# A softmax over rows: ScalarE's exponential loops with one row a turn instead of five, and a shorter general path

## Chip, cores and metric

The kernel runs on one core of one Trainium2 chip. The metric is the device time of one execution in microseconds (us), taken as the median of several executions. The profile is a hardware trace of one execution.

## What is computed

A softmax with temperature 2 over the last axis of a float32 array of 16 x 1024 x 512, which the kernel treats as 16384 rows of 512 values:

```python
def reference(x: np.ndarray) -> np.ndarray:
    temp = 2.0
    x_scaled = x / temp
    x_max = np.max(x_scaled, axis=-1, keepdims=True)
    exp_x = np.exp(x_scaled - x_max)
    return (exp_x / np.sum(exp_x, axis=-1, keepdims=True)).astype(np.float32)
```

The input is drawn from a normal distribution. 33.55 MB are read and 33.55 MB are written.

## The kernel before

The 16384 rows lie on 128 partitions, so that each partition has 128 rows of 512 values ("row" means one such row of all partitions from here on). They are moved in ten tiles of 3, 5 and then eight times 15 rows. An arena in SBUF holds 98 rows; the first eight tiles fill it, and the last two go where tiles 0 to 3 were, once those are stored.

The fast path leaves the subtraction of the maximum out: ScalarE computes exp(0.5 x) in place, with the sum of each row as a second output, VectorE takes the reciprocal of the sums and multiplies, and SyncE stores. At the end VectorE and TensorE count how many sums lie between 1 and 1e30. If all do, the kernel is done; if not, a general path computes everything again with the maximum subtracted. With this input the general path's loops are not entered.

```python
TILES = [
    (3, 0), (5, 3), (15, 8), (15, 23), (15, 38), (15, 53), (15, 68), (15, 83), (15, 0), (15, 15),
]
LATE = {8: (0, 1, 2), 9: (3,)}     # tiles 8 and 9 are loaded when these are stored
ARENA = 98
HEAD = [3]
E = 5
TURN = 83
...
    def take(eng, sem, n):
        eng.wait_ge(sem, n).then_inc(sem, -n)
...
        # VectorE: one pair of instructions per tile, five rows at a time in the last tile
        for j, ks in enumerate(pairs):
            b, c = starts[ks[0]], sum(sizes[k] for k in ks)
            a = b % ARENA
            nc.vector.reciprocal(
                out=recip[:, b : b + c], in_=stats[:, b : b + c]
            )._wait_ge(s_exp, ks[-1] + 1).then_inc(s_rec, 1)
            nc.vector.tensor_mul(
                out=arena[:, a : a + c],
                in0=arena[:, a : a + c],
                in1=recip[:, b : b + c].unsqueeze(2).to_broadcast([P, c, D]),
            )._wait_ge(s_rec, j + 1).then_inc(s_mul, 1)
...
        # TensorE's queue waits for each load and tells ScalarE how many chunks it brought
        for t in range(len(tiles)):
            nc.tensor.wait_ge(ld[t], 48 if t == SPREAD else 16).then_inc(s_go, owner.count(t))
...
        nc.scalar.preload_act_table(Exp)
        for k, c in enumerate(HEAD):
            take(nc.scalar, s_go, 1)
            for b in range(starts[k], starts[k] + c):
                ins = nc.scalar.activation(
                    out=arena[:, b], in_=arena[:, b], func=Exp, scale=0.5,
                    accum_out=stats[:, b : b + 1],
                )
            ins.then_inc(s_exp, 1)
        exponentials(straight, TURN)            # rows 3 to 82
        for t, us in LATE.items():              # the loads of tiles 8 and 9
            nc.scalar.wait_ge(s_home[t], landings(us))
            load(nc.scalar, t)
        exponentials(TURN, n_rows)              # rows 83 to 127

        for t in range(len(tiles)):
            store(nc.sync, t)
...
    def exponentials(first, end):
        row = nc.scalar.alloc_register(f"row{first}")
        nc.scalar.reg_mov(row, first)
        with nc.scalar.While(lambda: nc.scalar.snap(row, min_val=first, max_val=end) < end):
            now = nc.scalar.snap(row, min_val=first, max_val=end - E)
            take(nc.scalar, s_go, 1)
            at = nc.s_assert_within(
                now % ARENA, 0, ARENA - E,
                skip_runtime_bounds_check_because="no chunk reaches over the arena's end",
            )
            for r in range(E):
                data = arena[:, r : ARENA - E + 1 + r][:, bass.ds(at, 1)]
                ins = nc.scalar.activation(
                    out=data, in_=data, func=Exp, scale=0.5,
                    accum_out=stats[:, r : n_rows - E + 1 + r][:, bass.ds(now, 1)],
                )
            ins.then_inc(s_exp, 1)
            nc.scalar.reg_add(row, row, E)
```

The loads of tiles 1 to 7 are issued by ScalarE ahead of all this, the load of tile 0 by SyncE. The general path of before works on 64 rows at a time, with a loop of one ACTIVATE a row on ScalarE.

Of the kernel before, what the change touches and what calls it, by code (L numbers as in the profile page):

```python
# [13 lines left out]
LATE = {8: (0, 1, 2), 9: (3,)}  # L14
ARENA = 98

HEAD = [3]
E = 5

SPREAD = 1  # L20

TURN = 83

LO, HI = 1.0, 1.0e30
G = 64
# [3 lines left out]
def kernel(  # L29
# [5 lines left out]
    nc = tc.nc  # L35
# [3 lines left out]
    Exp = mybir.ActivationFunctionType.Exp  # L39
    Alu = mybir.AluOpType  # L40
# [3 lines left out]
    N, D = xf.shape  # L44
    P = nc.NUM_PARTITIONS
    n_rows = N // P
    assert sum(r for r, _ in TILES) == n_rows

    arena = nc.alloc_sbuf_tensor("arena", (P, ARENA, D), fp32)
    stats = nc.alloc_sbuf_tensor("stats", (P, n_rows), fp32)  # L50
# [4 lines left out]
    flag = nc.alloc_sbuf_tensor("flag", (1, 1), mybir.dt.int32)  # L55
# [15 lines left out]
        _, r, at = tiles[t]  # L71
        return arena[:, at : at + r, :]

    straight = sum(HEAD)
    sizes = HEAD + [E] * ((n_rows - straight) // E)
    starts = [sum(sizes[:k]) for k in range(len(sizes))]
    assert sum(sizes) == n_rows
    owner = [max(t for t, (b, _, _) in enumerate(tiles) if b <= s) for s in starts]
    assert all(s + c <= sum(tiles[t][:2]) for s, c, t in zip(starts, sizes, owner))


    pairs = []
    for k, t in enumerate(owner):
        most = 1 if t == len(tiles) - 1 else 3
        if pairs and len(pairs[-1]) < most and owner[pairs[-1][0]] == t:
            pairs[-1].append(k)
        else:
            pairs.append([k])
    upto = [1 + max(j for j, ks in enumerate(pairs) if owner[ks[0]] == t) for t in range(len(tiles))]

    ld = [nc.alloc_semaphore(f"ld{t}") for t in range(len(tiles))]
    s_home = {t: nc.alloc_semaphore(f"s_home{t}") for t in LATE}
# [11 lines left out]
    g_go = nc.alloc_semaphore("g_go")  # L104
    g_top = nc.alloc_semaphore("g_top")
    g_st = nc.alloc_semaphore("g_st")
    g_neg = nc.alloc_semaphore("g_neg")
    g_exp = nc.alloc_semaphore("g_exp")
    g_rec = nc.alloc_semaphore("g_rec")
    g_mul = nc.alloc_semaphore("g_mul")  # L110
# [27 lines left out]
    def take(eng, sem, n):  # L138
        eng.wait_ge(sem, n).then_inc(sem, -n)  # L139

    def rounds(eng, body, step=1):

        last = n_rows // G
        i = eng.alloc_register("tile")
        eng.wait_ge(s_near, 16)
        eng.wait_ge(s_flag, 1)
        eng.reg_load(i, flag[0:1, 0:1])
        with eng.While(lambda: eng.snap(i, min_val=0, max_val=last) < last):  # L150
            body(eng.snap(i, min_val=0, max_val=last - 1))
            eng.reg_add(i, i, step)

    def early():
        load(nc.sync, 0)
# [5 lines left out]

    def program():

        for j, ks in enumerate(pairs):
            b, c = starts[ks[0]], sum(sizes[k] for k in ks)
            a = b % ARENA
            nc.vector.reciprocal(  # L167
                out=recip[:, b : b + c], in_=stats[:, b : b + c]
            )._wait_ge(s_exp, ks[-1] + 1).then_inc(s_rec, 1)
            nc.vector.tensor_mul(  # L170
                out=arena[:, a : a + c],
                in0=arena[:, a : a + c],
                in1=recip[:, b : b + c].unsqueeze(2).to_broadcast([P, c, D]),
            )._wait_ge(s_rec, j + 1).then_inc(s_mul, 1)

        nc.gpsimd.memset(ones[:, :], 1.0).then_inc(s_ones, 1)  # L176
        nc.gpsimd.tensor_scalar(  # L177
            out=inside[:, :], in0=stats[:, :], scalar1=LO, scalar2=HI,
            op0=Alu.max, op1=Alu.min,
        )._wait_ge(s_exp, len(sizes)).then_inc(s_cnt, 1)  # L180
        nc.vector.scalar_tensor_tensor(  # L181
            out=inside[:, :], in0=inside[:, :], scalar=1.0, in1=stats[:, :],
            op0=Alu.mult, op1=Alu.is_equal, accum_out=count[:, :],
        )._wait_ge(s_cnt, 1).then_inc(s_cnt, 1)
        nc.vector.tensor_scalar(  # L185
            out=flag[:, :], in0=total[:, :], scalar1=float(N), scalar2=float(n_rows // G),
            op0=Alu.is_ge, op1=Alu.mult,
        )._wait_ge(s_tot, 1).then_inc(s_flag, 1)


        for t in range(len(tiles)):
            nc.tensor.wait_ge(ld[t], 48 if t == SPREAD else 16).then_inc(s_go, owner.count(t))
        nc.tensor.wait_ge(s_ones, 1)
        nc.tensor.matmul(  # L194
            total[:, :], lhsT=count[:, :], rhs=ones[:, :], start=True, stop=True
        )._wait_ge(s_cnt, 2).then_inc(s_tot, 1)

        nc.scalar.preload_act_table(Exp)  # L198
        for k, c in enumerate(HEAD):
            take(nc.scalar, s_go, 1)  # L200
            for b in range(starts[k], starts[k] + c):
                ins = nc.scalar.activation(  # L202
                    out=arena[:, b], in_=arena[:, b], func=Exp, scale=0.5,
                    accum_out=stats[:, b : b + 1],
                )
            ins.then_inc(s_exp, 1)
        exponentials(straight, TURN)
        for t, us in LATE.items():
            nc.scalar.wait_ge(s_home[t], landings(us))
            load(nc.scalar, t)  # L210
        exponentials(TURN, n_rows)

        for t in range(len(tiles)):
            store(nc.sync, t)

        x_g = xf.rearrange("(t p r) d -> t p r d", p=P, r=G)
        o_g = of.rearrange("(t p r) d -> t p r d", p=P, r=G)
        data = arena[:, 0:G]  # L220

        def vector(_):
            for i in range(n_rows // G):
                nc.vector.reduce_max(
                    out=g_max[:, :], in_=data, axis=mybir.AxisListType.X, negate=True
                )._wait_ge(g_go, i + 1).then_inc(g_top, 1)
                nc.vector.reciprocal(
                    out=g_sum[:, :], in_=g_sum[:, :]
                )._wait_ge(g_exp, G * (i + 1)).then_inc(g_rec, 1)

        def scalar(_):
            take(nc.scalar, g_neg, 1)
            row = nc.scalar.alloc_register("g_row")
            nc.scalar.reg_mov(row, 0)
            with nc.scalar.While(lambda: nc.scalar.snap(row, min_val=0, max_val=G) < G):
                now = nc.scalar.snap(row, min_val=0, max_val=G - 1)
                nc.scalar.activation(
                    out=data[:, bass.ds(now, 1)], in_=data[:, bass.ds(now, 1)], func=Exp,
                    scale=0.5, bias=g_max[:, bass.ds(now, 1)], accum_out=g_sum[:, bass.ds(now, 1)],
                ).then_inc(g_exp, 1)  # L240
                nc.scalar.reg_add(row, row, 1)

        def gpsimd(_):
            nc.gpsimd.wait_ge(s_end, at_end)
            for i in range(n_rows // G):
                nc.gpsimd.dma_start(out=data, in_=x_g[i]).then_inc(g_ld, 16)
                nc.gpsimd.wait_ge(g_ld, 16 * (i + 1)).then_inc(g_go, 1)
                nc.gpsimd.tensor_scalar_mul(
                    out=g_max[:, :], in0=g_max[:, :], scalar1=0.5
                )._wait_ge(g_top, i + 1).then_inc(g_neg, 1)  # L250
                nc.gpsimd.tensor_mul(
                    out=data, in0=data, in1=g_sum[:, :].unsqueeze(2).to_broadcast([P, G, D])
                )._wait_ge(g_rec, i + 1).then_inc(g_mul, 1)
                nc.gpsimd.wait_ge(g_mul, i + 1)
                nc.gpsimd.dma_start(out=o_g[i], in_=data).then_inc(g_st, 16)
                nc.gpsimd.wait_ge(g_st, 16 * (i + 1))

        rounds(nc.vector, vector, n_rows // G)
        rounds(nc.scalar, scalar)
        rounds(nc.gpsimd, gpsimd, n_rows // G)  # L260
        nc.sync.wait_ge(s_near, 16)
        nc.sync.wait_ge(s_end, at_end)

    def exponentials(first, end):
        row = nc.scalar.alloc_register(f"row{first}")
        nc.scalar.reg_mov(row, first)
        with nc.scalar.While(lambda: nc.scalar.snap(row, min_val=first, max_val=end) < end):  # L267
            now = nc.scalar.snap(row, min_val=first, max_val=end - E)  # L268
            take(nc.scalar, s_go, 1)
            at = nc.s_assert_within(  # L270
                now % ARENA, 0, ARENA - E,
                skip_runtime_bounds_check_because="no chunk reaches over the arena's end",
            )
            for r in range(E):
                data = arena[:, r : ARENA - E + 1 + r][:, bass.ds(at, 1)]
                ins = nc.scalar.activation(  # L276
                    out=data, in_=data, func=Exp, scale=0.5,
                    accum_out=stats[:, r : n_rows - E + 1 + r][:, bass.ds(now, 1)],
                )
            ins.then_inc(s_exp, 1)  # L280
            nc.scalar.reg_add(row, row, E)

    here = str(nc.cur_bb)
    entry, rest = nc.main_func.blocks[0], list(nc.main_func.blocks[1:])
# [42 lines left out]
```

## Time and profile before

| | |
|---|---|
| median time | 159.96 us (lowest 159.89) |
| span of the profiled execution | 158.7 us |
| ScalarE busy | 80.6 us (51%) |
| VectorE busy | 73.2 us (46%) |
| moved by DMA | 67.12 MB, mean 423 GB/s over the span |
| idle time of ScalarE until a load had landed | 55.6 us |

An engine's busy time counts its data instructions; register, branch and semaphore instructions of its sequencer are recorded, but not counted as busy. "L276" is line 276 of the kernel. A name with q at its end (ACTq, SPq) is an engine's sequencer. Times are from the start of the span.

### The profile page before, as it was taken

The numbers are of one execution on the slowest core, as the hardware profiler recorded it, in microseconds if no ns is written. First come the engines' busy times: TensorE is split into PE (matmuls) and PEld (weight loads), VectorE is DVE, ScalarE is ACT, GpSimd is POOL, SyncE is SP. The second block draws the span as 40 slices with busy tenths as digits, with TensorE's granted clock in tenths as the row PEclk, the third lists the DMA queues.
The fourth block names the chain that finished last, engine by engine and source line by source line (L and its number), as shares of the span: only waits on it lengthen the run. The fifth ranks groups of instructions, "written<-read, shape, count | busy, mean of one in ns | idle before, by whom it ended". The sixth has DMA issues, their size and how long they took to land. (4 is left out here: it accounts for less than half of the span.)

```text
span 158.7 us, 659 instructions
## 1 busy us (share of the span) xinstructions
PE 0.2 (0%) x2; PEld 0.1 (0%) x2; DVE 73.2 (46%) x27; ACT 80.6 (51%) x257; POOL 0.9 (1%) x6
## 2 busy tenths in 40 slices
PE   0000000000000000000000000000000000000000
PEld 0000000000000000000000000000000000000000
DVE  0047001992981990059500991049700793796000
ACT  0590498697498009940399007950199205980000
POOL 0000000000000000000000000000000000010000
DMA  7999999989899999999999999999999999999995
GB/s 265 395 480 401 454 407 363 501 372 501 387 472 395 472 395 465 403 457 410 457 410 457 410 441 426 443 426 441 426 434 434 434 434 434 434 434 434 410 449 256
DMA packets 3025, 67.12 MB, mean 423 GB/s; under 512 B 336, under 2 KB 336, under 8 KB 720
## 3 DMA queue, kind: packets, MB, share of 16 engines
q1 hardware_dynamic: 1584, 34.34, 50.5%
q10 hardware_dynamic: 1440, 32.77, 48.5%
q14 instruction: 1, 0.01, 0.0%
HBM read 33.55 MB, written 33.55 MB: 423 GB/s over the span
## 5 line engine op out<-in xcount | busy, mean ns | idle before, releaser
L276 ACT ACTIVATE arena<-arena x125 | 76.6, 614 | 55.6 <-ACTq L139 55.6
L170 DVE TENSOR_TENSOR arena<-arena,recip 128x7680 f32<-128x7680 f32 (+2 forms) x12 | 70.2, 5847 | 0.4
L167 DVE RECIPROCAL recip<-stats 128x15 f32<-128x15 f32 (+2 forms) x12 | 2.7, 224 | 71.9 <-ACT arena L276 62.7
L276 ACT ACTIVATION_READ_ACCUMULATOR arena<-arena x125 | 23.3, 186 | 0.0
L198 ACT ACT_TABLE_LOAD x1 | 1.3, 1283 | 5.8 <-issue 5.8
L202 ACT ACTIVATE arena<-arena 128x512 f32<-128x512 f32 x3 | 1.9, 618 | 0.0
L177 POOL TENSOR_SCALAR inside<-stats 128x128 f32<-128x128 f32 x1 | 0.6, 634 | 139.4 <-ACT arena L276 139.4
L202 ACT ACTIVATION_READ_ACCUMULATOR arena<-arena 128x1 f32 x3 | 0.6, 187 | 0.0
L194 PE MATMUL total<-ones,count 128*1 128x1 f32 x2 | 0.2, 164 | 145.4 <-DVE inside L181 145.4
L181 DVE SCALAR_TENSOR_TENSOR inside<-inside,stats 128x128 f32<-128x128 f32 x1 | 0.3, 285 | 0.0
L185 DVE TENSOR_SCALAR flag<-total 1x1 int32<-1x1 f32 x1 | 0.1, 146 | 0.3 <-PE total L194 0.3
L194 PEld LDWEIGHTS total<-ones,count 128*1 128x1 f32 x2 | 0.1, 80 | 145.4 <-DVE inside L181 145.4
L176 POOL MEMSET ones<- 128x1 f32 x1 | 0.1, 98 | 2.2 <-POOLq L37 2.2
L311 POOL MEMSET const-bfloat16-1.0<- 128x1 bf16 x1 | 0.1, 102 | 0.0
L311 POOL MEMSET const-uint8-127<- 128x1 uint8 x1 | 0.1, 102 | 0.0
L311 POOL MEMSET const-float32-0.0<- 128x1 f32 x1 | 0.1, 99 | 0.2 <-issue 0.2
L311 POOL MEMSET const-float32-1.0<- 128x1 f32 x1 | 0.1, 99 | 0.0
L181 DVE DVE_READ_ACCUMULATOR inside<-inside,stats 128x1 f32 x1 | 0.1, 83 | 0.0
## 6 DMA issues: line engine op xcount, KB each, us to landing
arena<-in_x_dram ACTq DMA_DIRECT2D x8, 3840.0 KB, 42.9
out_dram<-arena SPq DMA_DIRECT2D x8, 3840.0 KB, 27.4
out_dram<-arena SPq DMA_DIRECT2D x1, 1280.0 KB, 23.5
arena<-in_x_dram ACTq DMA_DIRECT2D x1, 1024.0 KB
arena<-in_x_dram SPq DMA_DIRECT2D x1, 768.0 KB, 5.5
out_dram<-arena SPq DMA_DIRECT2D x1, 768.0 KB, 15.3
arena<-in_x_dram ACTq DMA_DIRECT2D x1, 252.0 KB
arena<-in_x_dram ACTq DMA_DIRECT2D x1, 4.0 KB
```

Source lines behind the costliest of these rows:

```text
L167: nc.vector.reciprocal(out=recip[:, b : b + c], in_=stats[:, b : b + c])._wait_ge(s_exp, ks[-1] + 1).then_inc(s_rec, 1)
L170: nc.vector.tensor_mul(out=arena[:, a : a + c], in0=arena[:, a : a + c], in1=recip[:, b : b + c].unsqueeze(2).to_broadcast([P, c, D]),)._w ...
L176: nc.gpsimd.memset(ones[:, :], 1.0).then_inc(s_ones, 1)
L177: nc.gpsimd.tensor_scalar(out=inside[:, :], in0=stats[:, :], scalar1=LO, scalar2=HI, op0=Alu.max, op1=Alu.min,)._wait_ge(s_exp, len(sizes) ...
L181: nc.vector.scalar_tensor_tensor(out=inside[:, :], in0=inside[:, :], scalar=1.0, in1=stats[:, :], op0=Alu.mult, op1=Alu.is_equal, accum_ou ...
L185: nc.vector.tensor_scalar(out=flag[:, :], in0=total[:, :], scalar1=float(N), scalar2=float(n_rows // G), op0=Alu.is_ge, op1=Alu.mult,)._wa ...
L194: nc.tensor.matmul(total[:, :], lhsT=count[:, :], rhs=ones[:, :], start=True, stop=True)._wait_ge(s_cnt, 2).then_inc(s_tot, 1)
L198: nc.scalar.preload_act_table(Exp)
L202: ins = nc.scalar.activation(out=arena[:, b], in_=arena[:, b], func=Exp, scale=0.5, accum_out=stats[:, b : b + 1],)
L276: ins = nc.scalar.activation(out=data, in_=data, func=Exp, scale=0.5, accum_out=stats[:, r : n_rows - E + 1 + r][:, bass.ds(now, 1)],)
L311: nc = _bacc.Bacc("TRN2", target_bir_lowering=False, num_devices=1)
```

## The change

The change makes ScalarE's program shorter, from 76 instructions to 48:

- The two loops of the fast path take one row a turn, not five. The semaphore from the loads to ScalarE counts rows, and so does the one from ScalarE to VectorE.
- The first three rows, which stood as instructions of their own, go into the first loop.
- VectorE's chunks are written down directly (a tile each, five rows each in the last tile). Their shapes and order are the same as before.
- In the general path ScalarE does 64 rows in one ACTIVATE, without a loop. For that GpSimd adds the negative maximum to the data first, and VectorE sums the rows. The loops run zero times or once.

```diff
-HEAD = [3]
 E = 5
...
+    chunks = []
+    for t, (b, r, _) in enumerate(tiles):
+        c = r if t < len(tiles) - 1 else E
+        assert r % c == 0
+        chunks += [(t, b + o, c) for o in range(0, r, c)]
...
-            )._wait_ge(s_exp, ks[-1] + 1).then_inc(s_rec, 1)
+            )._wait_ge(s_exp, b + c).then_inc(s_rec, 1)
...
-        )._wait_ge(s_exp, len(sizes)).then_inc(s_cnt, 1)
+        )._wait_ge(s_exp, n_rows).then_inc(s_cnt, 1)
...
-            nc.tensor.wait_ge(ld[t], 48 if t == SPREAD else 16).then_inc(s_go, owner.count(t))
+            nc.tensor.wait_ge(ld[t], 48 if t == SPREAD else 16).then_inc(s_go, tiles[t][1])
...
         nc.scalar.preload_act_table(Exp)
-        for k, c in enumerate(HEAD):
-            take(nc.scalar, s_go, 1)
-            for b in range(starts[k], starts[k] + c):
-                ins = nc.scalar.activation(
-                    out=arena[:, b], in_=arena[:, b], func=Exp, scale=0.5,
-                    accum_out=stats[:, b : b + 1],
-                )
-            ins.then_inc(s_exp, 1)
-        exponentials(straight, TURN)
+        exponentials(0, TURN)
...
-        def scalar(_):
-            take(nc.scalar, g_neg, 1)
-            row = nc.scalar.alloc_register("g_row")
-            ...
+        def scalar():
+            for i in range(n_rows // G):
+                nc.scalar.activation(out=data, in_=data, func=Exp, scale=0.5)._wait_ge(
+                    g_sub, i + 1
                 ).then_inc(g_exp, 1)
...
-            now = nc.scalar.snap(row, min_val=first, max_val=end - E)
+            now = nc.scalar.snap(row, min_val=first, max_val=end - 1)
             take(nc.scalar, s_go, 1)
-            at = nc.s_assert_within(
-                now % ARENA, 0, ARENA - E,
-                skip_runtime_bounds_check_because="no chunk reaches over the arena's end",
-            )
-            for r in range(E):
-                data = arena[:, r : ARENA - E + 1 + r][:, bass.ds(at, 1)]
-                ins = nc.scalar.activation(
-                    out=data, in_=data, func=Exp, scale=0.5,
-                    accum_out=stats[:, r : n_rows - E + 1 + r][:, bass.ds(now, 1)],
-                )
-            ins.then_inc(s_exp, 1)
-            nc.scalar.reg_add(row, row, E)
+            data = arena[:, bass.ds(now % ARENA, 1)]
+            nc.scalar.activation(
+                out=data, in_=data, func=Exp, scale=0.5, accum_out=stats[:, bass.ds(now, 1)]
+            ).then_inc(s_exp, 1)
+            nc.scalar.reg_add(row, row, 1)
```

More of the change, by code (lines that the diff above doesn't have):

```diff
@@ L72, in sb @@
         return arena[:, at : at + r, :]
[L74 to L89, printed above, removed]
+    chunks = []
[3 more added lines that the diff above has]
+        chunks += [(t, b + o, c) for o in range(0, r, c)]
+    upto = [1 + max(j for j, c in enumerate(chunks) if c[0] == t) for t in range(len(tiles))]
     ld = [nc.alloc_semaphore(f"ld{t}") for t in range(len(tiles))]
@@ L106 @@
     g_st = nc.alloc_semaphore("g_st")
-    g_neg = nc.alloc_semaphore("g_neg")
+    g_sub = nc.alloc_semaphore("g_sub")
+    g_add = nc.alloc_semaphore("g_add")
     g_exp = nc.alloc_semaphore("g_exp")
@@ L139, in take, with rounds @@
         eng.wait_ge(sem, n).then_inc(sem, -n)
-    def rounds(eng, body, step=1):
-        last = n_rows // G
-        i = eng.alloc_register("tile")
+    def rounds(eng, body):
+        i = eng.alloc_register("general")
         eng.wait_ge(s_near, 16)
@@ L149, in rounds @@
         eng.reg_load(i, flag[0:1, 0:1])
-        with eng.While(lambda: eng.snap(i, min_val=0, max_val=last) < last):
-            body(eng.snap(i, min_val=0, max_val=last - 1))
-            eng.reg_add(i, i, step)
+        with eng.While(lambda: eng.snap(i, min_val=0, max_val=1) < 1):
+            body()
+            eng.reg_add(i, i, 1)
     def early():
@@ L162, in program @@
     def program():
-        for j, ks in enumerate(pairs):
-            b, c = starts[ks[0]], sum(sizes[k] for k in ks)
+        for j, (_, b, c) in enumerate(chunks):
             a = b % ARENA
@@ L185, in program @@
         nc.vector.tensor_scalar(
-            out=flag[:, :], in0=total[:, :], scalar1=float(N), scalar2=float(n_rows // G),
-            op0=Alu.is_ge, op1=Alu.mult,
+            out=flag[:, :], in0=total[:, :], scalar1=float(N), scalar2=None, op0=Alu.is_ge,
         )._wait_ge(s_tot, 1).then_inc(s_flag, 1)
         for t in range(len(tiles)):
-            nc.tensor.wait_ge(ld[t], 48 if t == SPREAD else 16).then_inc(s_go, owner.count(t))
+            nc.tensor.wait_ge(ld[t], 48 if t == SPREAD else 16).then_inc(s_go, tiles[t][1])
         nc.tensor.wait_ge(s_ones, 1)
@@ L220, in program, with vector @@
         data = arena[:, 0:G]
-        def vector(_):
+        def vector():
             for i in range(n_rows // G):
@@ L226, in vector, with gpsimd @@
                 )._wait_ge(g_go, i + 1).then_inc(g_top, 1)
+                nc.vector.reduce_sum(
+                    out=g_sum[:, :], in_=data, axis=mybir.AxisListType.X
+                )._wait_ge(g_exp, i + 1).then_inc(g_add, 1)
                 nc.vector.reciprocal(
                     out=g_sum[:, :], in_=g_sum[:, :]
-                )._wait_ge(g_exp, G * (i + 1)).then_inc(g_rec, 1)
-        def scalar(_):
-            take(nc.scalar, g_neg, 1)
-            row = nc.scalar.alloc_register("g_row")
[L234 to L239, printed above, removed]
+                )._wait_ge(g_add, i + 1).then_inc(g_rec, 1)
+        def scalar():
+            for i in range(n_rows // G):
+                nc.scalar.activation(out=data, in_=data, func=Exp, scale=0.5)._wait_ge(
+                    g_sub, i + 1
                 ).then_inc(g_exp, 1)
-                nc.scalar.reg_add(row, row, 1)
-        def gpsimd(_):
+        def gpsimd():
             nc.gpsimd.wait_ge(s_end, at_end)
@@ L247, in gpsimd @@
                 nc.gpsimd.wait_ge(g_ld, 16 * (i + 1)).then_inc(g_go, 1)
-                nc.gpsimd.tensor_scalar_mul(
-                    out=g_max[:, :], in0=g_max[:, :], scalar1=0.5
-                )._wait_ge(g_top, i + 1).then_inc(g_neg, 1)
+                nc.gpsimd.tensor_add(
+                    out=data, in0=data, in1=g_max[:, :].unsqueeze(2).to_broadcast([P, G, D])
+                )._wait_ge(g_top, i + 1).then_inc(g_sub, 1)
                 nc.gpsimd.tensor_mul(
@@ L256, in gpsimd @@
                 nc.gpsimd.wait_ge(g_st, 16 * (i + 1))
-        rounds(nc.vector, vector, n_rows // G)
+        rounds(nc.vector, vector)
         rounds(nc.scalar, scalar)
-        rounds(nc.gpsimd, gpsimd, n_rows // G)
+        rounds(nc.gpsimd, gpsimd)
         nc.sync.wait_ge(s_near, 16)
```

## Prediction

> **What bounds the kernel now.** I read the page first, for which engine is full. Its slices (40 of 4 us each, busy share in tenths) show two half-empty compute engines and full DMA engines:
>
> ```profile
> span 158.7 us, 659 instructions
> ...
> DVE  0047001992981990059500991049700793796000
> ACT  0590498697498009940399007950199205980000
> ...
> DMA  7999999989899999999999999999999999999995
> ```
>
> ScalarE and VectorE have holes in every tile; the DMA row has none except in the first and the last slice. So I cut the span where transfers begin and end (columns: stretch, length, busy time of PE, PEld, DVE, ACT, POOL, TensorE clock, DMA share, GB/s):
>
> ```profile
> 0.00:1.00 1.00, 0.00 (x0) 0.00 (x0) 0.00 (x0) 0.00 (x0) 0.20 (x4) 1.00 0.00 0
> 1.00:2.00 1.00, 0.00 (x0) 0.00 (x0) 0.00 (x0) 0.00 (x0) 0.00 (x0) 1.00 0.92 283
> ...
> 11.00:132.40 121.40, 0.00 (x0) 0.00 (x0) 61.93 (x17) 66.14 (x214) 0.00 (x0) 1.00 1.00 431
> 132.40:157.40 25.00, 0.19 (x2) 0.09 (x2) 9.40 (x9) 9.30 (x30) 0.63 (x1) 1.00 1.00 433
> 157.40:158.70 1.30, 0.00 (x0) 0.00 (x0) 0.00 (x0) 0.00 (x0) 0.00 (x0) 1.00 0.01 0
> ```
>
> The first load is issued at 0.00, data moves from 1.0 us on, and until 157.4 the share is 1.00; then 1.3 us pass until the last landing is known. The kernel moves 67.12 MB; 156.4 us of it gives 429 GB/s, and no stretch is left in which more could be moved. The time is bytes over rate plus 1.0 us before and 1.3 us after. A change in ScalarE's program moves it only if it makes the DMA engines run dry, or changes those two ends.
>
> Next, what ScalarE's rows cost (the groups of instructions, columns: busy us and mean ns of one, then the idle time before them and its releaser):
>
> ```profile
> L276 ACT ACTIVATE arena<-arena x125 | 76.6, 614 | 55.6 <-ACTq L139 55.6
> L170 DVE TENSOR_TENSOR arena<-arena,recip 128x7680 f32<-128x7680 f32 x7 | 57.1, 8158 | 0.2
> L276 ACT ACTIVATION_READ_ACCUMULATOR arena<-arena x125 | 23.3, 186 | 0.0
> ```
>
> An exponential is an ACTIVATE of 0.614 us and a read of its sum of 0.186 us, which overlap their neighbours: in the timeline one row follows the next every 0.61 us, also across a turn of the loop. The 55.6 us idle are waits for loads (L139 is the wait on `s_go`). Last, the end, from the timeline and, for the loop's sequencer work, the chain of waits (start, length, what; L276 here is the register operation ahead of an activation, L267 the loop's test):
>
> ```profile
> 141.86 0.19 ACT L276 ACTIVATION_READ_ACCUMULATOR arena<-arena  x1
> ...
> 142.31 2.83 DVE L170 TENSOR_TENSOR arena<-arena,recip 128x2560 f32<-128x2560 f32 x1
> ...
> 145.16 0.33 SPq L136 DMA_DIRECT2D out_dram<-arena  x1
> ```
>
> ```profile
> 132.95 0.07 ACTq L276
> ...
> 133.12 0.07 ACTq L276
> ...
> 133.60 0.04 ACTq L267
> ...
> 133.81 0.03 ACTq L267
> ...
> 134.07 0.10 ACTq L276
> ...
> 134.26 0.07 ACTq L276
> ```
>
> [...] the loop's test at 133.60 to 133.87 lies beside an ACTIVATE that runs from 133.38 to 133.99, and no gap follows. [...] here the step from the first test to what follows it is 133.60 to 133.81, so 0.21 us for both[...]. [...] the sum of loads and stores stays at 431 to 433 GB/s here, whether both queues are active or stores alone[...].
>
> **The change, part by part.**
>
> *Turns of one row.* Before, a turn does five rows, so 25 turns and three rows without a loop; after, 128 turns. The sequencer's work of a turn of one row, from the chain above: register operation to next one 0.19 (134.07 to 134.26), then the add to the row register and the step from it, about 0.06 (as between the close steps of that chain), then from the first test to the next turn's register operation 0.47 (133.60 to 134.07; test, jump, test, copy of the row, wait on `s_go`). Sum 0.72 us in the second loop, where the arena index wraps. In the first loop the wraparound costs less: in tile 5 the wait on `s_go` starts at 59.6 and again at 60.9,
>
> ```profile
> L139 ACTq EVENT_SEMAPHORE  x2: 17/17/17, 59.6 to 60.9; - x2
> ```
>
> so a turn of five rows took 1.3 us of sequencer, four of its rows at 0.16 to 0.17 (132.95 to 133.12), which leaves 0.63 to 0.65 for a turn of one row. The engine needs 0.61 a row. So a turn of one row is just no longer hidden: the row's period becomes the larger of the two, 0.63 in the first loop and 0.72 in the second.
>
> *First loop, rows 0 to 82.* A tile of 15 rows lasts 14 x 0.02 = 0.3 us longer. Loads land every 18.1 us (ScalarE waits 8.9 us ahead of each of these tiles), ScalarE takes 9.2 and VectorE 8.4, so there is room. The store of a tile goes out 0.3 us later; but stores in mid-run take some 34 us from issue to landing, of which 18 is their own share, so each waits about 16 us behind another. Hidden. The loads of the last two tiles are issued by ScalarE after this loop, at 84.1. There the sequencer was some 3.5 us ahead of the engine; it will no longer be, so I expect 87.5. They are needed when the load before them has moved its data, just before it lands at 95.8 (issue at 5.3 and 90.5 us). Hidden, with 7 us to spare.
>
> *Second loop, the last tile.* This is the only place near the path. Its load lands at 132.4, and its store of 3.93 MB, issued at 145.16, ends the kernel. After: the fifteenth row ends 14 x (0.72 - 0.61) = 1.5 us later, at 143.5 in place of 142.0. VectorE's three chunks of 3.06 us had just kept pace with five rows of 3.06; with rows of 0.72 the third chunk starts at once after the fifteenth row and ends 3.05 us later, at about 146.7. So the last store is issued 1.5 us later. How much of that shows? The store's 3.93 MB at 433 GB/s take 9.1 us and end at 157.4, so its data begins at 148.3, behind the store before it. An issue on idle engines was followed by data after 1.0 us (first cut of the span). So issue at 147.3 would do: 2.1 us of slack, against 1.5 us. Hidden, with 0.6 us left.
>
> *No separate first rows.* ScalarE's first row starts at 7.10 after its table load (5.81 to 7.09), which waits behind nine DMA issues. The new loop's head, some 0.3 us of sequencer work, falls in the table load. Zero. Stores of the first two tiles go out up to 0.2 us later; loads keep the engines full.
>
> *VectorE, stores, loads.* Instruction by instruction the same shapes and order; only line numbers and the thresholds of the waits differ, in rows rather than chunks. *General path*: runs only when a sum is out of bounds, so here no instruction of it runs. Fewer instructions to fetch: nothing in the chain waits for a fetch. Zero.
>
> Sum: 0.0 on the path, plus a small allowance of 0.05: 160.0 us.
>
> **Rivals.** First, the sequencer doesn't run ahead over a branch, so that each turn's 0.47 us stands beside 0.61: rows of 1.1 us, a last tile 14 x 0.47 = 6.6 us longer, less 2.1 of slack, so 164.5. For it: per-row loops are the change's whole price. Against it: the timeline of before has no gap at any of its turns. Second, the turn is dearer than my 0.72 (a longer jump, a row's wait not ready): at 0.80 the store goes out 2.7 us later, and 0.6 us shows, 160.6. Third, the short loop jumps faster, so that rows come at 0.63 in both loops: the same 160.0, which only the trace would tell from my reading. Fourth, a shorter program starts sooner: against it, the first data moves at 1.0 us after two DMA issues that no part of the change touches. Fifth, ScalarE's later stores let loads run ahead, the balance of the queues shifts, and the rate with it; in the two mixes seen it is 431 and 433, so under 0.5%.
>
> **Range and chances.** The centre is 160.0. Below there is only scatter: 159.5. Above, the thin slack of 0.6 us can be used up by some turns of 0.75 to 0.80: 160.8. A slowdown of over 2%, 3.2 us, needs rows of 1.0 us, which is the first rival; I give it 3 in 100. A gain of over 2% would need the DMA engines to move faster: 1 in 100.
>
> **What would show it.** ACTIVATE still about 0.61 us, but row starts 0.63 apart up to row 82 and 0.72 in the last two or three tiles; ScalarE's wait for loads shorter by 0.3 to 1.5 us a tile; the loads of the last two tiles issued near 87.5; the last store near 146.7; DMA share 1.00 without a hole between 147 and 149. Wrong if the DMA share drops ahead of the last store, or if rows come at 1 us or more.

## The result and the profile after

The changed kernel takes 160.72 us against 159.93 us, each the median of six executions; the ratio is 1.0047, with a 95% interval of 1.0031 to 1.0063. A second set gave 160.57 against 159.90 us and 1.0046 (1.0033 to 1.0059). Some executions of most of these kernels take 5 to 14 us longer than the others of the same program; the ratios leave them out, and so do the medians of the second set and of the table below. So the loss is real, but small, some 0.7 us, and lies within the predicted range; the predicted centre, 160.0, was too low by most of it. The profile shown here is that of the second set, an execution of 160.57 us.

From its page (slices of 4 us, busy share in tenths; then the groups of instructions, with busy us, mean ns, and idle time before them):

```profile
span 159.2 us, 1279 instructions
...
DVE  0047001993971990059500990029800694787000
ACT  0590598796598009930499008970299305990000
...
DMA  7999998989898989898989898989899999999994
...
L247 ACT ACTIVATE arena<-arena x128 | 80.1, 627 | 53.3 <-ACTq L130 53.2
...
L247 ACT ACTIVATION_READ_ACCUMULATOR arena<-arena x128 | 24.0, 187 | 0.0
```

The program is shorter, yet the trace has 1279 instructions where it had 659: one row a turn means that the loop's own instructions run 128 times instead of 25. ScalarE's idle time until loads land fell from 55.6 to 53.3 us only, and VectorE is as before. The stretches of transfers, cut as before (ACT is the fourth busy column; the last three numbers are TensorE clock, DMA share and GB/s):

```profile
1.00:2.00 1.00, 0.00 (x0) 0.00 (x0) 0.00 (x0) 0.00 (x0) 0.00 (x0) 1.00 0.95 283
11.00:132.40 121.40, 0.00 (x0) 0.00 (x0) 61.29 (x17) 68.72 (x215) 0.00 (x0) 1.00 1.00 430
```

430 GB/s where it was 431, and the start is the same. So the 0.7 us is neither in the start nor in a visibly lower rate. The end, from the timeline:

```profile
142.85 0.19 ACT L247 ACTIVATION_READ_ACCUMULATOR arena<-arena  x1
143.07 0.19 DVE L155 RECIPROCAL recip<-stats 128x5 f32<-128x5 f32 x1 [0.29 <-ACT arena L247]
...
143.29 2.83 DVE L158 TENSOR_TENSOR arena<-arena,recip 128x2560 f32<-128x2560 f32 x1
...
146.14 0.33 SPq L127 DMA_DIRECT2D out_dram<-arena  x1
```

The last store is issued at 146.14 instead of 145.16, 0.98 us later. That is close to the loss, so it was the first suspect ("the end theory" below: the late store leaves the DMA engines without work ahead of its data); the next view speaks against it. After that issue there is no hole in the DMA engines:

```profile
146.14:147.00 0.86, 0.19 (x2) 0.09 (x2) 0.33 (x3) 0.00 (x0) 0.00 (x0) 1.00 0.83 357
147.00:148.00 1.00, 0.00 (x0) 0.00 (x0) 0.00 (x0) 0.00 (x0) 0.00 (x0) 1.00 1.14 492
148.00:149.00 1.00, 0.00 (x0) 0.00 (x0) 0.00 (x0) 0.00 (x0) 0.00 (x0) 1.00 1.15 492
149.00:150.00 1.00, 0.00 (x0) 0.00 (x0) 0.00 (x0) 0.00 (x0) 0.00 (x0) 1.00 1.14 492
```

(A transfer is counted where it starts, hence shares a little under or over 1; laid beside each other by start and end, 15 to 17 transfers of data are under way at every moment from 144 to 157 us.)

What differs is the very end. Cut where the last transfers of the last store start, before:

```profile
156.90:157.10 0.20, 0.00 (x0) 0.00 (x0) 0.00 (x0) 0.00 (x0) 0.00 (x0) 1.00 0.71 307
157.10:157.40 0.30, 0.00 (x0) 0.00 (x0) 0.00 (x0) 0.00 (x0) 0.00 (x0) 1.00 0.00 0
157.40:157.70 0.30, 0.00 (x0) 0.00 (x0) 0.00 (x0) 0.00 (x0) 0.00 (x0) 1.00 0.02 0
```

and after:

```profile
156.90:157.10 0.20, 0.00 (x0) 0.00 (x0) 0.00 (x0) 0.00 (x0) 0.00 (x0) 1.00 0.00 0
157.10:157.40 0.30, 0.00 (x0) 0.00 (x0) 0.00 (x0) 0.00 (x0) 0.00 (x0) 1.00 0.00 0
157.40:157.70 0.30, 0.00 (x0) 0.00 (x0) 0.00 (x0) 0.00 (x0) 0.00 (x0) 1.00 0.26 103
```

After, no large transfer starts from 156.9 to 157.4, and then a single one does: 103 GB/s for 0.3 us is 31 KB, one transfer of 30720 bytes on one of the 16 DMA engines. Before, the last two started ahead of 157.1. So 15 engines finish as early as before, and one finishes late. The trace has 16 landing times for each load and store of a whole tile. Read as one of each of the 16 engines, they give the lag of the slowest engine. At the last store:

```
                     eighth engine   last engine   last after eighth
before                  157.93 us      158.64 us        0.71 us
after                   157.88 us      159.17 us        1.29 us
```

The eighth is no later. The whole difference, 0.53 us between these two executions (160.57 and 160.04 us), is one engine's. It falls behind little by little: for the loads of the last three tiles the lag is 0.47, 0.65 and 0.84 us after, against 0.28, 0.60 and 0.57 us before.

The single transfers in the trace show where the lag comes from. From 44 us on, each of them starts within 13 ns of the end of another, so they can be strung into 16 sequences, one for each DMA engine. A transfer of 30720 bytes takes 1.138 us nearly always (before, all but 41 of 1598 from then on are within 3 ns of it). After, 51 of them take longer (by more than 3 ns; 1.25 us in all), and all 51 lie in one sequence, the one that ends last, at 158.69 us; the other 15 end by 157.86 us. Before, 40 take longer, by 0.54 us in all, besides one beside a fetch of instructions. The difference, 0.71 us, is the loss to within 0.05 us. In both executions the last landing follows 0.48 us after the end of the last sequence (158.16 and 158.64 us before), as it would if it were that engine's.

### The profile page after: what moved, and what is told of

The parts are those of the page before. It is cut to its first block, busy times and chain, and to the rows that moved or that the text cites. A ratio compares the mean times of both kernels' runs of the same rounds, so it can differ in the third digit from the quotient of the medians.

```text
span 170.5 us, 1279 instructions
## 1 busy us (share of the span) xinstructions
PE 0.2 (0%) x2; PEld 0.1 (0%) x2; DVE 73.2 (43%) x27; ACT 83.8 (49%) x257; POOL 0.9 (1%) x6
## 5 line engine op out<-in xcount | busy, mean ns | idle before, releaser
L247 ACT ACTIVATE arena<-arena x128 | 80.1, 626 | 64.2 <-ACTq L130 64.2
L247 ACT ACTIVATION_READ_ACCUMULATOR arena<-arena x128 | 23.8, 186 | 0.0
```

Source lines behind the costliest of these rows:

```text
L247: nc.scalar.activation(out=data, in_=data, func=Exp, scale=0.5, accum_out=stats[:, bass.ds(now, 1)]).then_inc(s_exp, 1)
```

## Experiments

All are compared with the kernel before on the same chip. "Lag" is the time from the eighth to the last engine at the last store, in the profiled execution.

| kernel | instructions in the trace | median, us | ratio to before (95%) | lag, us |
|---|---|---|---|---|
| before | 659 | 159.89 to 159.92 | 1 | 0.71 |
| changed, again | 1279 | 160.57 | 1.0046 (1.0033 to 1.0059) | 1.29 |
| second loop only | 875 | 160.25 | 1.0023 (1.0013 to 1.0033) | 1.07 |
| first loop only | 1063 | 160.24 (once) | none | none |
| last store delayed | 660 | 159.88 | 0.9998 (0.9989 to 1.0007) | 0.58 |
| GpSimd loop, 155 turns | 1282 | 160.17 | 1.0019 (1.0011 to 1.0026) | 0.90 |
| GpSimd loop, 465 turns | 2522 | 167.27 | 1.046 (1.0447 to 1.0474) | 2.67 |
| no loops on ScalarE | 387 | 160.10 | 1.0014 (1.0007 to 1.0021) | 0.91 |
| more waits on ScalarE | 909 | 160.22 | 1.003 (1.0016 to 1.0045) | 0.74 |
| changed, two rows split | 1279 | 161.18 | 1.0082 (1.0069 to 1.0095) | 1.34 |
| before, two rows split | 659 | 160.77 | 1.0049 (1.0034 to 1.0064) | 1.40 |
| changed, three rows split | 1279 | 161.49 | 1.0097 (1.0082 to 1.0112) | 1.77 |
| changed, no row split | 1277 | 160.68 | 1.0048 (1.0035 to 1.0062) | see text |

### The changed kernel again, and its loops one at a time

The first was the changed kernel as it is.

> The changed kernel once more. First theory (the end): rows come 0.62 us apart up to row 82 and 0.67 in the last three tiles, the last store is issued about 0.8 us later than the 145.16 us of before, and the DMA engines show a hole of about 0.7 us just ahead of that store's data, so the time is 0.6 to 0.8 us above before. Rival (the rate): no such hole, but the DMA engines' bytes from 11 to 132 us go slower or the load of the last tile lands some 0.6 us later than the 132.41 us of before. My prediction's own step (2.1 us of slack) would have the time equal to that of before.

The pace of the rows was as the end theory had it, and so, nearly, was the time of the last store (0.98 us later, about 0.8 expected); its hole was not there. The load of the last tile landed at 132.62, 0.2 us later than before, as its slowest engine lagged more (0.84 against 0.57 us).

Second loop only, on top of the changed kernel (`exponentials` gets the number of rows of a turn; the first three rows stand alone):

```diff
-        exponentials(0, TURN)
+        take(nc.scalar, s_go, 3)
+        for b in range(3):
+            nc.scalar.activation(...).then_inc(s_exp, 1)
+        exponentials(3, TURN, E)
```

> Only rows 83 to 127 one a turn; the first three rows stand alone and rows 3 to 82 go five a turn. The end theory: all of the loss is here, ratio to before 1.004 to 1.005. The rival (first rows, first loop, the rate in mid-run): ratio 1.000 to 1.001.

It costs 0.35 us, half of the loss, where the end theory wanted all of it. So part of the loss belongs to the first loop or the first rows, which are far from the end.

First loop only:

```diff
-        exponentials(TURN, n_rows)
+        exponentials(TURN, n_rows, E)
```

> Only rows 0 to 82 one a turn, rows 83 to 127 five a turn. The end theory: as before, ratio 0.999 to 1.001, last store at about 145.2 us. The rival (first rows, first loop, the rate in mid-run): ratio 1.004 to 1.005.

There is only one time for it, 160.24 us. That is 0.35 us above before, in line with halves that add up, but a single execution has no interval, and nothing rests on it.

### The last store alone

```diff
             a = b % ARENA
+            if j == len(pairs) - 1:
+                nc.vector.reciprocal(out=pad[:, 0:b], in_=stats[:, 0:b])
             nc.vector.reciprocal(
```

> The kernel before with one useless reciprocal of 128x123 (about 0.9 us on VectorE, into a tensor that nothing reads) ahead of the last chunk's reciprocal, so that the last store is issued about 0.9 us later and nothing else changes. No slack (the end theory): time up by 0.8 to 0.9 us, ratio 1.005 to 1.006. My predicted slack of 2.1 us: ratio 1.000. A slack in between shows as the part of 0.9 us that is missing.

The timeline of this kernel around the added work:

```profile
142.02 0.92 DVE L171 RECIPROCAL pad<-stats 128x123 f32<-128x123 f32 x1
142.85 0.13 DVE L172 RECIPROCAL recip<-stats 128x5 f32<-128x5 f32 x1
143.02 2.83 DVE L175 TENSOR_TENSOR arena<-arena,recip 128x2560 f32<-128x2560 f32 x1
```

and of its store:

```profile
145.87 0.33 SPq L138 DMA_DIRECT2D out_dram<-arena  x1
```

The store went out 0.71 us later, not 0.9, as the added work overlaps its neighbours and VectorE had reached it a little sooner. That cost nothing: ratio 0.9998. The end theory is out, as is any other in which the last store's issue sets the end at this size of delay; at least 0.7 us of slack is there, and the changed kernel, 0.98 us later, still shows no hole.

### Instructions that do nothing

If neither the rows' pace nor the stores matter, what is left of the change is that sequencers execute more instructions. A loop on GpSimd, which has nothing to do from 2.7 to 142 us, tests that alone (the helper that holds it is written out here):

```diff
         nc.gpsimd.memset(ones[:, :], 1.0).then_inc(s_ones, 1)
+        n = nc.gpsimd.alloc_register("idle")
+        nc.gpsimd.reg_mov(n, 0)
+        with nc.gpsimd.While(lambda: nc.gpsimd.snap(n, min_val=0, max_val=155) < 155):
+            nc.gpsimd.reg_add(n, n, 1)
```

> The kernel before, with a loop of 155 empty turns (about four register and branch instructions each, some 620 in all) on GpSimd, which is idle from 2.6 to 142 us; it touches no data, no semaphore and no other engine. Third theory (instructions as such): each instruction that a sequencer executes holds up one of the 16 DMA engines a little, about 1.1 ns an instruction from the 620 more that the changed kernel executes for 0.7 us; then the time rises by 0.4 to 0.8 us, ratio 1.003 to 1.005. Rival (ScalarE's rows and its stores come later, or its counting down of the semaphore of the loads): ratio 1.000.

It costs 0.3 us (0.19%, interval 0.11 to 0.26%), with the rest of the kernel unchanged: its ScalarE and its stores are those of before. That is a clear effect, but half of what the same number of instructions costs on ScalarE; the table below shows why. With three times as many turns:

> The same with 465 turns, some 1860 instructions. Instructions as such: three times as much, 1.5 to 2.2 us, ratio 1.010 to 1.014. Rival: ratio 1.000.

The time of this one can't be used, and that is my mistake in sizing it: a turn took 0.345 us, longer than I had reckoned with, so GpSimd was late for its own part at the end:

```profile
163.16 0.63 POOL L184 TENSOR_SCALAR inside<-stats 128x128 f32<-128x128 f32 x1 [160.42 <-issue]
```

Its DMA engines can be used. In each of these stretches one more transfer of data starts, at 157.83 and at 159.01 us, both on the last engine; the other 15 have no data to move after 158.02 us:

```profile
157.70:158.00 0.30, 0.00 (x0) 0.00 (x0) 0.00 (x0) 0.00 (x0) 0.00 (x0) 1.00 0.26 102
158.00:160.50 2.50, 0.00 (x0) 0.00 (x0) 0.00 (x0) 0.00 (x0) 0.00 (x0) 1.00 0.03 12
```

The last landing is at 160.67 instead of 158.64 us, 2.0 us later, and the lag at that store is 2.67 us, with the second last engine at 0.41. So 1863 more empty instructions cost one engine 2.0 us. The single transfers show how. In this kernel, from 70 to 78 us, when ScalarE executes nothing and GpSimd 93 instructions, four transfers take 0.02 to 0.06 us longer, 0.145 us together. Before, there is one in these 8 us, of 0.02. In the changed kernel ScalarE executes some 58 instructions per 4 us while it has rows, and the longer transfers lie where it does: none from 51 to 57 and from 69 to 75 us, when it waits. And in the kernel with 155 turns, whose loop is over at 56 us, they are as rare as before from 60 to 76 us (0.03 us in all, against 0.04).

Added up from 40 us on, over all transfers of 30720 bytes (what they take over 1.138 us, without the one beside a fetch), against the instructions executed from then on:

| kernel | instructions from 40 us on | transfers longer by, us | time over before, us |
|---|---|---|---|
| before | 433 | 0.57 | 0 |
| changed, again | 865 | 1.25 | 0.67 |
| second loop only | 649 | 1.00 | 0.35 |
| last store delayed | 434 | 0.48 | -0.02 |
| GpSimd loop, 155 turns | 623 | 0.83 | 0.28 |
| GpSimd loop, 465 turns | 1809 | 2.57 | 2.03 (last landing) |
| no loops on ScalarE | 239 | 0.34 | 0.21 |
| more waits on ScalarE | 613 | 0.80 | 0.33 |

(The last two are explained next.) Each instruction more or less than before is worth 1.2 to 2.0 ns here, on ScalarE as on GpSimd, with a scatter of some 0.1 us in a single trace. That is why GpSimd's 620 instructions cost half as much: only some 190 of them are executed after 40 us, but some 430 of ScalarE's 620. Ahead of that no such cost is seen: from 28 to 36 us no transfer of 30720 bytes is longer, neither before (58 instructions) nor with 465 turns (151).

The other way round, no loops at all:

```diff
-        with nc.scalar.While(...):
-            ...
+        for t, b, c in [(t, b, r) for t, (b, r, _) in enumerate(tiles) if first <= b < end]:
+            take(nc.scalar, s_go, c)
+            for now in range(b, b + c):
+                data = arena[:, now % ARENA]
+                nc.scalar.activation(out=data, in_=data, func=Exp, scale=0.5,
+                                     accum_out=stats[:, now : now + 1]).then_inc(s_exp, 1)
```

> The changed kernel without loops on ScalarE: 128 exponentials with fixed addresses, one wait on the loads a tile, so no register or branch instructions; its program is longer to fetch. Instructions as such: some 340 instructions fewer than before, so 0.2 to 0.4 us faster than before (ratio 0.9975 to 0.999), limited by the next slowest DMA engine. Rival (pace of the rows): rows at 0.61 us as before, so ratio 1.000.

It has only 387 instructions in the trace and yet is slower than before, by 0.2 us. The list of DMA queues on its page has the reason; before, that line read "q14 instruction: 1, 0.01, 0.0%", and in the changed kernel there is no such line:

```profile
q1 hardware_dynamic: 1584, 34.34, 50.4%
q10 hardware_dynamic: 1440, 32.77, 48.4%
q14 instruction: 2, 0.02, 0.0%
```

The longer program is fetched with two transfers of 8192 bytes, 0.31 us each, which one of the 16 engines takes besides its share (at 22.0 and 88.8 us). Its lag is 0.40 us at the load that lands before the second fetch and 0.95 us at the next one after it. So the fetch ate what the missing instructions gave: 0.34 us of longer transfers in place of 0.57, by the table. The same time with a single fetch was not measured.

Last, more instructions on ScalarE at an unchanged pace of 0.612 us a row:

```diff
             for r in range(E):
+                for _ in range(4):
+                    nc.scalar.wait_ge(s_ones, 1)
                 data = arena[:, r : ARENA - E + 1 + r][:, bass.ds(at, 1)]
```

> The kernel before, with four waits on a semaphore that is long set (s_ones) ahead of each row in ScalarE's loops, 500 instructions more; turns, rows' pace of 0.61 us and the counting down stay as they are. Instructions as such: 0.4 to 0.6 us more, ratio 1.0025 to 1.004. Rival (pace of the rows): ratio 1.000, as the rows come no later. If only this one and not the GpSimd loops cost time, it is something of ScalarE's own sequencer.

Only 250 instructions were added, not 500: the trace has two waits a row in place of four. The ratio, 1.003 with a wide interval (1.0016 to 1.0045), says slower, with rows as quick as before; the lag of its profiled execution, 0.74 us, is hardly above that of before, and that execution was the shortest of this kernel (160.11 us). In it, the transfers are longer by 0.22 us more than before for 180 instructions after 40 us. It supports the reading, but carries little by itself.

### Which engine lags

Tile 1 is loaded in parts: of its last row 126 and 2 partitions are loaded apart. In the trace of before, the transfers of 2048 bytes of that row show strings of nine, most of them started 80 ns apart, and 14 times nine is 126: by this estimate two of the 16 engines get less. That the lagging one is among them was a guess. Four kernels move more rows, or none, into those parts:

```diff
-            parts = [(0, P, 0, r - 1), (0, 126, r - 1, r), (126, P, r - 1, r)]
+            parts = [(0, P, 0, r - 2), (0, 126, r - 2, r), (126, P, r - 2, r)]
```

> The changed kernel, with the last two rows of tile 1, not only the last one, split into 126 and 2 partitions. That takes another 16 KB, about 0.6 us, from two of the 16 DMA engines. The theory that the loss is one DMA engine that lags (the last one done 1.3 us after the eighth, at the last store) and that it is one of those two: the lag falls to about 0.7 us, the time by 0.5 to 0.6 us, to 160.0. Rival (the lagging engine is another one, or the end isn't set by it): 160.6 or a little more, since 14 engines get 1 KB more each.

> The same in the kernel before, where the last DMA engine is done 0.7 us after the eighth and the second last 0.5 us. Lagging-engine theory: at most 0.2 to 0.3 us faster, since engines that aren't relieved end 0.3 us later than the eighth; ratio 0.998 to 0.9995. Rival: 1.000 to 1.0005.

> The changed kernel with three rows of tile 1 split so. Lagging-engine theory: relief of 1.2 us against a lag of 1.3, so all engines end nearly together; 159.7 to 159.9, as fast as the kernel before or a little faster. Rival: 160.6 to 160.7.

All three are slower, by 0.6 and 0.9 us against the changed kernel and by 0.8 us against the one before. The times don't tell which engine lags, though, because the split also delays all engines near the start: the load of tile 2 has landed from the eighth engine at 17.93, 18.04 (changed) and 17.82 us (before), where it was 17.00 and 17.18, and at the last store the eighth engine is still 0.4 to 0.7 us later. The 16 sequences tell more: in each of the three, two engines end at least 0.4 us ahead of the others, as engines with less to do would, while the lag at the last store is no smaller than in the kernel it started from. So the lagging engine doesn't seem to be one that the split relieves. Nor does it help to split no row:

```diff
-SPREAD = 1
+SPREAD = None
```

> The changed kernel with tile 1 loaded in one piece, no row of it split off. With two rows split the time rose by 0.6 us and with three by 0.9, so the lagging DMA engine is one of those that the split gives more to. If that goes on to zero rows: 0.3 to 0.6 us faster than the changed kernel, 160.0 to 160.3, and the last engine done 0.7 to 1.0 us after the eighth. If the split's two relieved engines set the end without it: 160.6 or more.

1.0048 (1.0035 to 1.0062) is the changed kernel's own ratio. (Its profiled execution took 162.24 us, 1.6 us above the median of this kernel, and had several late engines, so its lag isn't given.) With two rows split in the changed kernel, the engine with the longer transfers ends at 158.07 us, and another one last, at 159.25, with more transfers to do; with three, the one with the longer transfers (1.42 us in all from 43 us on) is the last again, at 159.83. So the shares of the 16 engines move the end by tenths of a us too; which of the 16 the instructions hold up stays unknown.

## Why the prediction was right, and where it missed

**The bound.** Right: bytes over rate, 430 GB/s, and two fixed ends. It treated the 16 DMA engines as one, though; the end is that of the slowest of them (last landing at 158.64 us of a span of 158.7 before, at 159.17 of 159.2 after).

**Turns of one row.** Right in kind, too high for the second loop. Row starts are 0.624 us apart in the first loop (0.63 to 0.65 was worked out) and 0.668 in the second (0.72). The term that was off is the step from the first test: in the changed loop it takes 0.15 us, where I had 0.21 from the second loop of before (the first loop there had 0.15, which the chain I read did not show). From the chain of waits (L243 is the loop's test):

```profile
142.41 0.04 ACTq L243
142.45 0.11 issue
142.56 0.03 ACTq L243
```

0.06 us less in a sum of 0.72 gives 0.66, which is what the rows show. The third rival, faster jumps, holds in part. The first (the sequencer waits at each branch, rows of 1.1 us) and the second (dearer turns) are out.

**First loop.** The loads of the last two tiles were issued at 87.15 us; 87.5 was expected. Hidden, as said.

**Last tile.** 14 x (0.668 - 0.612) gives 0.78 us, and the load landed 0.2 us later: 0.98, where 1.5 was expected. Hidden, as said, and the delayed store of the kernel before shows at least 0.7 us of the slack that had been put at 2.1; its full size wasn't measured.

**The sum.** "0.0 on the path, plus a small allowance of 0.05" is the step that failed: the measured term is 0.7 us. What was left out is that instructions which only turn a loop cost the DMA engines something. The prediction asked what each of them costs ScalarE, and whether ScalarE is on the path, and stopped there. The loops of empty instructions on GpSimd show the missing term without ScalarE: 0.3 us for 620 (by time), 2.0 us for 1860 (by the last landing). For ScalarE's 620 the time gives 0.7 us. That 160.72 lies in the range all the same is luck: its upper end, 160.8, stood for dearer turns that use up the slack of the last store, and neither came about; the same holds for the second rival's 160.6.

**Instructions to fetch.** "Nothing in the chain waits for a fetch. Zero" looked at the wrong thing too. The changed program does save the one fetch of 8192 bytes that the old one had at 102 us, and the fetch loads a DMA engine (for 0.31 us); but it saved nothing here, as another engine was the last one already before the change (158.16 us; the one with the fetch ended at 158.06).

**What stays open.** Why an executed instruction holds up one DMA engine, which of the 16 it is, and why nothing of it is seen from 28 to 36 us. No run here shows the way in which it does. Nor do these runs tell whether the 0.7 us would be there in an execution without a trace.

No kernel tried here is faster than the one before.

## What to carry to other kernels

When a kernel keeps all DMA engines busy from end to end, ask of every change what it puts on a single one of them: here the last of the 16 set the end, and the fetches of a longer program (two of 0.31 us) or the instructions of a tighter loop (0.71 us more of longer transfers, in the changed kernel) each cost some tenths of a microsecond, though no compute engine was on the path. A program that is shorter to store can be longer to run (48 instructions of ScalarE's in place of 76, but 1279 in the trace in place of 659): count instructions executed, not instructions written. And check slack by spending it: a delay added at one place told in one run what the likeness of two numbers, 0.98 us of delay and 0.7 us of loss, had made look settled.

## What the runs showed of the hardware that I had not expected

- For each instruction more that ScalarE's or GpSimd's sequencer executed from 40 us on, the transfers of 30720 bytes took 1.2 to 2.0 ns longer in sum (1.25 us for 865 instructions, 0.57 for 433), mostly as single ones that took up to 0.06 us longer than their 1.138 us; in the changed kernel all of them, from 44 us on, were on one of the 16 DMA engines.
- The step from a loop's first test over its jump took 0.15 us in the first loop and 0.21 in the second loop of the same program (before); in the changed kernel's second loop it took 0.15.
- Splitting one or two rows of one tile more cost 0.6 to 0.9 us of 160; the next tile's load came 0.6 to 1.0 us later on the eighth engine.
